# A fused two-block decoder kernel on one core: the top-k stage keeps the larger weight ring, its transposes and gate sums stand later, and the one-hots are laid out by four tokens

## The chip, the cores and the metric

The kernel runs on one NeuronCore of a Trainium2 chip. It is one launch. The metric is the time of one execution on the device in microseconds; less is better. TensorE (PE) does the matmuls, VectorE (DVE), ScalarE (ACT) and GpSimd (POOL) work beside it, and SyncE (SP) issues the transfers from memory.

## The reference, cut to what matters

The program is two transformer blocks over 256 tokens with 1024 channels. The change lies in the first block's feed-forward layer, which picks 16 of 16384 experts for each of 8 heads of a token:

```
q = (xt @ w_query).reshape(T, 8, 2, 128)
s = einsum('thpd,hpkd->thpk', q, subkeys)      # 128 scores per head and half
sv, si = lax.top_k(s, 16)
cand    = (sv[:, :, 0, :, None] + sv[:, :, 1, None, :]).reshape(T, 8, 256)
cand_id = (si[:, :, 0, :, None] * 128 + si[:, :, 1, None, :]).reshape(T, 8, 256)
top_s, pos = lax.top_k(cand, 16)
expert = take_along_axis(cand_id, pos, -1)
gate   = softmax(top_s, -1)
act = gelu(einsum('thkd,td->thk', u_tab[expert], xt), approximate=False)
out = einsum('thk,thkd->td', gate * act, v_tab[expert])
```

All of it is in float32.

## The kernel before, in words

The kernel gathers no experts. It computes the activations of all 16384 experts for all tokens (`peer_u`), builds from each token's 128 pairs of indices and gates a 128 x 128 matrix of gates (`peer_g`), multiplies the two, and multiplies the result with the whole value table (`peer_v`).

*Float32 on PE.* Each weight tile of 128 x 1024 comes by one transfer into a `raw` buffer; ACT rounds it into `hi` (L106), and DVE or POOL writes the rest, `lo = raw - hi` (L109). A product is three matmuls: hi with the high part of x, hi with the low part, lo with the high part (L255 to L257 in `ws`, where 256 tokens are the moving side; L196 to L198 and L898 with 512 columns). `lo_pattern` says which engine subtracts: `V` for DVE, `G` for POOL, `VG` in turns. The buffers stand in rings: 3 raw, 4 hi and 4 lo, and while `open_wx` holds the extra pool open 3 raw, 1 hi and 1 lo more.

*Stages around the change.* The output projection of the attention part ends with additions into `h` (L266), the norm of each token tile (L274 to L322), transposes (L334) and the split of x into xTh and xTl (L289). Then follow `peer_query` (about 142 to 190 us of the profiled span), the top-k stage (to 392), the gate stage (to 633), and the value stage in two calls of `peer_v` (to 815 and to 994). Ahead of `peer_query` the kernel closes the extra pool, and opens it again for the second call of `peer_v`.

*Top-k stage.* `merge` interleaves two generators by steps: `peer_topk` and `peer_u` for the first 64 of 128 groups of experts. A weight quarter is 128 x 2048, two halves of 24 matmuls each. All subtractions are POOL's here. For each token tile of 128 tokens, `peer_topk` computes scores (L749, four PSUM banks of the tag `sm`), picks 16 of 128 for sixteen head halves, adds candidates, picks 16 of 256 for eight heads (all DVE), and finds the indices of the picked by comparing with 0 to 15 (L792), multiplying with the indices (L795) and summing (L797). Then comes the gates' exponential (L800, ACT), their sum, reciprocal and product (L804 to L806, DVE), three transposes into one `sm` bank (L811 to L813), and copies into `sel` (L814, ACT) and `gate` (L815, DVE).

*Gate stage.* `peer_g` takes eight tokens at a time. Two one-hots E of shape [128 keys x 8 tokens], bf16, come from comparing `sel` with an iota (L852, DVE). For each four tokens ACT copies one into A (L857) and DVE multiplies the other with the gates into B (L858), both float32 in the storage of `h`. Four matmuls A x B give the gate matrices (L862), and L868 (DVE) and L870 (ACT) put them into the activations, which `peer_u` goes on computing for the experts 64 to 127 (L828, L830). In this stage and the value stage the subtractions alternate between DVE and POOL. The lines in which A and B are written are

```
A, B = [h[q].rearrange("p (n t j) -> p n t j", n=2, t=T2)[:, i] for q in range(2)]
a.activation(A, E[0][:, :, u:u + T2].rearrange("p j t -> p t j"), AF.Copy)
v.tensor_tensor(B, E[1][:, :, u:u + T2].rearrange("p j t -> p t j"),
                gate[:, t0:t0 + T2, None].to_broadcast([P, T2, P]), op=ALU.mult)
```

*Order of work.* Each engine runs its instructions in the order in which the tile scheduler puts them, and that order depends on the code's order, on the buffers, and on the scheduler's estimate of times.

## Time and profile before

| what | value |
|---|---|
| time, three runs | 1699.96, 1701.71, 1703.58 us (median 1701.71) |
| the profiled execution | 1688.16 us, its span 1686.3 us |
| granted TensorE clock, mean | 0.996 |
| PE busy | 1631.9 us, 97% |
| DVE busy | 1191.6 us, 71% |
| ACT busy | 948.1 us, 56% |
| POOL busy | 430.0 us, 25% |

The span goes from the first to the last instruction of the profiled execution; that execution's own time is 1.9 us longer. Waits of an engine are no busy time. Shares are means over all stages; the sections behind look at single stages.

### The profile page before, as it was taken

The page shows a single profiled execution, that of the slowest core. Times are in us where ns is not written, and L with a number is a line of the kernel's source. Part 1 is how long each engine was busy: PE and PEld are TensorE (multiplying, and loading weights), DVE is VectorE, ACT ScalarE, POOL GpSimd, SP SyncE. Part 2 cuts the span into 40 slices and gives each one's busy share as a digit, 9 for nine tenths or more (in the row PEclk, how much of TensorE's full clock was granted, in tenths as well). Part 3 has the DMA queues.
Part 4 walks back from the last instruction along what each step waited for, and adds up shares of the span by engine and source line. Part 5 has one row for each costly group of instructions (what it writes and reads, how often), then busy time and mean ns, then how long its engine had stood idle before and what let it go on. Part 6 is the DMA issues. An engine that isn't in the chain of part 4 may idle for free.

```text
span 1686.3 us, 27635 instructions
## 1 busy us (share of the span) xinstructions
PE 1631.9 (97%) x10592; PEld 1451.6 (86%) x10592; DVE 1191.6 (71%) x2236; ACT 948.1 (56%) x1435; POOL 430.0 (25%) x191
## 2 busy tenths in 40 slices
PE   6999999899999999999999999999999989999998
PEld 5878999899999997888888879869998777799986
DVE  7766597906999995445444467878885676688846
ACT  5544545446676665555455557466664556566633
POOL 1000598974332324444444411100000000000000
PEclk9999999999999999999999999999999999999999
DMA  7425655454444446566765555436555652365551
GB/s 272 159 88 162 198 157 173 161 175 156 145 135 141 133 144 203 185 193 201 232 194 187 188 177 178 131 113 197 183 193 186 216 174 87 119 196 189 188 188 62
DMA packets 83199, 285.07 MB, mean 169 GB/s; under 512 B 10555, under 2 KB 14588, under 8 KB 82940
## 3 DMA queue, kind: packets, MB, share of 16 engines
q1 hardware_dynamic: 83068, 283.31, 52.1%
q8 instruction: 83, 1.36, 0.3%
q14 instruction: 48, 0.39, 0.1%
HBM read 281.16 MB, written 2.12 MB: 168 GB/s over the span
## 4 chain that ended last, share of the span: by engine, by line
PE 70%; DVE 23%; ACT 2%; issue 1%; DMA 1%; POOL 1%; SPq 0%; DVEq 0%; ACTq 0%; POOLq 0%
PE mm L898 21%; PE mm L256 9%; PE mm L255 9%; PE mm L257 9%; PE mm L196 6%; PE mm L198 6%; PE mm L197 6%; DVE h L858 6%; DVE lo L109 4%; DVE E L852 3%; DVE act L868 2%; POOL lo L109 1%; PE sm L553 1%; DVE xn L322 1%; PE sm L525 1%
## 5 line engine op out<-in xcount | busy, mean ns | idle before, releaser
L106 ACT ACTIVATE hi<-raw 128x1024 fp32r<-128x1024 f32 x513 | 543.3, 1061 | 371.1 <-PE mm L256 156.4
L109 DVE TENSOR_TENSOR lo<-raw,hi 128x1024 fp32r<-128x1024 f32 x353 | 434.7, 1233 | 190.7 <-ACT hi L106 182.6
L255 PE MATMUL mm<-xTh,hi 128*128 128x256 f32 x1992 | 563.5, 283 | 0.0
L257 PE MATMUL mm<-xTh,lo 128*128 128x256 f32 x1992 | 556.5, 279 | 4.4 <-POOL lo L109 4.3
L256 PE MATMUL mm<-xTl,hi 128*128 128x256 f32 x1992 | 556.8, 280 | 0.7 <-DVE xTl L289 0.7
L109 POOL TENSOR_TENSOR lo<-raw,hi 128x1024 fp32r<-128x1024 f32 x160 | 406.2, 2545 | 423.7 <-ACT hi L106 423.5
L257 PEld LDWEIGHTS mm<-xTh,lo 128*128 128x128 f32 x1992 | 375.0, 188 | 5.6 <-POOL lo L109 5.4
L256 PEld LDWEIGHTS mm<-xTl,hi 128*128 128x128 f32 x1992 | 375.4, 188 | 1.3 <-DVE xTl L289 1.1
L255 PEld LDWEIGHTS mm<-xTh,hi 128*128 128x128 f32 x1992 | 375.3, 188 | 1.1 <-issue 0.6
L858 DVE TENSOR_TENSOR h<-E,gate 128x512 f32<-128x512 bf16 x64 | 115.2, 1800 | 4.3 <-PE sm L862 4.3
L196 PE MATMUL mm<-hi,xTh 128*128 128x512 f32 x256 | 105.6, 413 | 1.9 <-DVE xTl L289 1.0
L197 PE MATMUL mm<-lo,xTh 128*128 128x512 f32 x256 | 103.0, 402 | 0.5 <-DVE lo L109 0.5
L198 PE MATMUL mm<-hi,xTl 128*128 128x512 f32 x256 | 102.4, 401 | 0.0
L289 DVE TENSOR_TENSOR xTl<-act,xTh 128x256 fp32r<-128x256 f32 x64 | 45.1, 711 | 80.1 <-PE mm L898 78.9
L289 DVE TENSOR_TENSOR wl<-act,wh 128x256 fp32r<-128x256 f32 x64 | 43.3, 683 | 80.7 <-PE mm L898 80.4
L857 ACT ACTIVATE h<-E 128x512 f32<-128x512 bf16 x64 | 73.2, 1143 | 40.8 <-DVE E L852 39.2
L1320 DVE SCALAR_TENSOR_TENSOR fc<-mm,cw,fc 128x255 f32<-128x255 f32 (+1 forms) x176 | 84.5, 480 | 3.1
L898 PE MATMUL mm<-hi,xTh 128*128 128x512 f32 x256 | 81.0, 396 | 1.6 <-DVE act L828 0.9
L898 PE MATMUL mm<-hi,xTl 128*128 128x512 f32 x256 | 80.9, 396 | 0.1
L898 PE MATMUL mm<-lo,xTh 128*128 128x512 f32 x256 | 80.8, 395 | 0.0
L898 PE MATMUL mm<-hi,wh 128*128 128x512 f32 x256 | 80.2, 395 | 0.0
L898 PE MATMUL mm<-hi,wl 128*128 128x512 f32 x256 | 80.2, 395 | 0.0
(298 smaller groups left out, 2376.7 us busy)
## 6 DMA issues: line engine op xcount, KB each, us to landing
raw<-in_peer_uT SPq DMA_DIRECT2D x128, 512.0 KB, 3.7
raw<-in_peer_v SPq DMA_DIRECT2D x128, 512.0 KB, 4.4
raw<-in_ffn_up_ws SPq DMA_DIRECT2D x88, 512.0 KB, 3.7
raw<-in_ffn_down_a SPq DMA_DIRECT2D x40, 512.0 KB, 4.2
raw<-in_w_in_xs SPq DMA_DIRECT2D x20, 512.0 KB, 5.2
raw<-in_ab_ws SPq DMA_DIRECT2D x16, 512.0 KB, 4.4
raw<-in_ple_gate_xs SPq DMA_DIRECT2D x16, 512.0 KB, 4.5
raw<-in_w_query_ws SPq DMA_DIRECT2D x12, 512.0 KB, 4.8
```

Of the source, the lines that this page charges most:

```text
L106: nc.scalar.activation(hi, raw, AF.Copy)
L109: eng.tensor_tensor(lo, raw, f32(hi), op=ALU.subtract)
L196: nc.tensor.matmul(p, xh[:, k, t], hi[:, w], start=n == 1 and kk == 0, stop=False)
L197: nc.tensor.matmul(p, xh[:, k, t], lo[:, w], start=False, stop=False)
L198: nc.tensor.matmul(p, xl[:, k, t], hi[:, w], start=False, stop=n == total[c] and kk == 1)
L255: nc.tensor.matmul(o, hi[:, w], xh[:, k, :], start=k == 0, stop=False)
L256: nc.tensor.matmul(o, hi[:, w], xl[:, k, :], start=False, stop=False)
L257: nc.tensor.matmul(o, lo[:, w], xh[:, k, :], start=False, stop=k == 7)
L289: self.nc.vector.tensor_tensor(dl, p, f32(dh), op=ALU.subtract)
L858: v.tensor_tensor(B, E[1][:, :, u:u + T2].rearrange("p j t -> p t j"), gate[:, t0:t0 + T2, None].to_broadcast([P, T2, P]), op=ALU.mult)
L898: nc.tensor.matmul(self.acc[tt][c], st_[:, t], mv[:, c * 512:c * 512 + 512], start=first and j == js[0] and i == 0, stop=j == last and i == 2)
L1320: v.scalar_tensor_tensor(c[:, o + sft:o + S], p[:, o:o + S - sft], cw[:, wi, j:j + 1], c[:, o + sft:o + S], op0=ALU.mult, op1=ALU.add)
```

## The change

The extra pool of the weight ring is kept through `peer_query`, closed, opened again for the top-k stage (with the storage of the activations on the other side of memory), and closed ahead of the gate stage. The transposes of a token tile, the gate sums before them and the copies behind them move into a function `finish`: tile 0's is called in the seventh of tile 1's first sixteen steps, tile 1's after 14 steps more. In `peer_g` an E holds [2 groups][128 keys][4 tokens], so that the part of four tokens is contiguous; A and B are read in that order and written with a step of 128 float32. The two halves of the value stage change places, and its subtractions are all DVE's (`lo_pattern` is `V`). The diff, with the lines that only move cut from it:

```diff
--- before.py
+++ after.py
@@ -28,7 +28,8 @@
 NW_AB = 7
 HOLD = 4
 NWT = 6
-TOPK_STEPS = 90
+TOPK_STEPS = 74
+TOPK_REST = 14
 D_N = 3, 4
 D_PQ = 2
 LAG = 2
@@ -679,31 +680,34 @@
             px = e(self.tc.tile_pool(name="px", bufs=1, reuse_waits="tile"))
             xT = self.xT
             sel = px.tile([P, 2, S], BF, name="sel"), px.tile([P, S], F32, name="gate")
-            pa = e(self.pool("pa"))
-            self.slots = [pa.tile([P, 64, S], F32, name="act0")]
             keep = e(self.tc.tile_pool(name="keep", bufs=1, space=bass.MemoryType.DRAM)).tile([2, P, D], F32, name="keep")
             for t in range(2):
                 nc.sync.dma_start(keep[t], h[t])
-            self.close_wx()
-            with self.pool("topk") as tk:
-                qT = self.peer_query(xT, tk)
-                self.flush()
-                self.np.close()
-                self.merge(self.peer_topk(qT, tk, *sel), self.peer_u(xT, 0, 4))
-            self.acc = None
-            with self.pool("pg") as pg:
-                self.slots.append(pg.tile([P, 64, S], F32, name="act1"))
+            with ExitStack() as sa:
+                with self.pool("topk") as tk:
+                    qT = self.peer_query(xT, tk)
+                    self.flush()
+                    self.close_wx()
+                    self.np.close()
+                    pa = sa.enter_context(self.tc.tile_pool(name="pa", bufs=1, side="right", reuse_waits="tile"))
+                    self.slots = [pa.tile([P, 64, S], F32, name="act0")]
+                    self.open_wx()
+                    self.merge(self.peer_topk(qT, tk, *sel), self.peer_u(xT, 0, 4))
+                self.close_wx()
+                self.acc = None
+                self.slots.append(e(self.pool("pg")).tile([P, 64, S], F32, name="act1"))
                 self.done = [64, 0]
                 self.u_pattern = "VG"
                 with self.pool("gp") as gp:
                     self.merge(self.peer_g(*sel, gp), self.peer_u(xT, 4, 8))
+                self.lo_pattern = "V"
                 for t in range(2):
                     nc.sync.dma_start(h[t], keep[t])
-                self.run(self.peer_v(range(64, 128), xT))
+                self.run(self.peer_v(range(64), xT))
             self.open_norm()
             self.open_wx()
             pv = e(self.pool("pv"))
-            self.run(self.peer_v(range(64), [pv.tile([P, NWT, S], F32R, name=n) for n in ("wh", "wl")],
+            self.run(self.peer_v(range(64, 128), [pv.tile([P, NWT, S], F32R, name=n) for n in ("wh", "wl")],
                                  hold=4, norm=self.T["mix_norm"][0]))
 
     def act(self, j):
@@ -740,6 +744,19 @@
         nc.sync.dma_start(io, T["c_io16"])
         skT = big().rearrange("p (a k) -> p a k", a=16)
         nc.sync.dma_start(skT, T["subkeysT"])
+
+        def finish(tt, ij, gt, g3):
+
+            sm = self.tiny.tile([P, 8], F32, tag="gsm", name=self.nm("gsm"))
+            v.tensor_reduce(sm, g3, axis=AX.X, op=ALU.add)
+            v.reciprocal(sm, sm)
+            v.tensor_tensor(g3, g3, sm[:, :, None].to_broadcast([P, 8, 16]), op=ALU.mult)
+            p = self.sm_ps()
+            for i, x in enumerate((ij[:, :P], ij[:, P:], gt)):
+                self.tc.keep_in_program_order(nc.tensor.transpose(p[:, i * P:(i + 1) * P], x, self.ident))
+            t = slice(tt * P, tt * P + P)
+            a.activation(sel[:, :, t], p[:, :2 * P].rearrange("p (q t) -> p q t", q=2), AF.Copy)
+            v.tensor_copy(gate[:, t], p[:, 2 * P:3 * P])
         for tt in range(2):
             s = big()
             for b in range(4):
@@ -751,6 +768,8 @@
                 a.activation(s[:, b * 512:(b + 1) * 512], p, AF.Copy)
             sv, si = small(), small(U32)
             for hp in range(16):
+                if tt and hp == 6:
+                    finish(0, *late)
                 o, x = hp * 16, s[:, hp * P:(hp + 1) * P]
                 v.max(sv[:, o:o + 8], x)
                 v.max_index(si[:, o:o + 8], sv[:, o:o + 8], x)
@@ -795,24 +814,13 @@
                 v.tensor_tensor(e4, e4, sf4[:, :, q, None, :].to_broadcast([P, 8, 16, 16]), op=ALU.mult)
                 yield
                 v.tensor_reduce(ij[:, q * P:(q + 1) * P], e3, axis=AX.X, op=ALU.add)
+                if not q:
+                    self.tc.keep_in_program_order(a.activation(gt, gt, AF.Exp))
                 yield
-
-            self.tc.keep_in_program_order(a.activation(gt, gt, AF.Exp))
-            for _ in range(2):
-                yield
-            sm = self.tiny.tile([P, 8], F32, tag="gsm", name=self.nm("gsm"))
...
-            v.tensor_copy(gate[:, t], p[:, 2 * P:3 * P])
+            late = ij, gt, g3
+        for _ in range(TOPK_REST):
+            yield
+        finish(1, *late)
 
     def peer_u(self, xT, n0, n1):
 
@@ -841,22 +849,22 @@
 
         nc, h = self.nc, self.h
         v, a = nc.vector, nc.scalar
-        T1, T2 = 8, 4
-        iota = pool.tile([P, P, T1], BF, name="iota")
-        nc.gpsimd.iota(iota, pattern=[[1, P], [0, T1]], base=0, channel_multiplier=0, allow_small_or_imprecise_dtypes=True)
+        T1, T2 = 2, 4
+        iota = pool.tile([P, P, T2], BF, name="iota")
+        nc.gpsimd.iota(iota, pattern=[[1, P], [0, T2]], base=0, channel_multiplier=0, allow_small_or_imprecise_dtypes=True)
         yield S // T2
-        for b in range(S // T1):
-            t = slice(b * T1, b * T1 + T1)
-            E = [pool.tile([P, P, T1], BF, tag=f"E{q}", name=self.nm("E")) for q in range(2)]
+        for b in range(0, S, T1 * T2):
+            E = [pool.tile([P, T1, P, T2], BF, tag=f"E{q}", name=self.nm("E")) for q in range(2)]
             for q in range(2):
-                v.tensor_tensor(E[q], sel[:, q, None, t].to_broadcast([P, P, T1]), iota, op=ALU.is_equal)
-            for u in range(0, T1, T2):
-                i = u // T2
-                t0 = b * T1 + u
+                x = sel[:, q, b:b + T1 * T2].rearrange("p (n t) -> p n t", n=T1)
+                v.tensor_tensor(E[q], x[:, :, None, :].to_broadcast([P, T1, P, T2]),
+                                iota[:, None].to_broadcast([P, T1, P, T2]), op=ALU.is_equal)
+            for i in range(T1):
+                t0 = b + i * T2
                 A, B = [h[q].rearrange("p (n t j) -> p n t j", n=2, t=T2)[:, i] for q in range(2)]
-                a.activation(A, E[0][:, :, u:u + T2].rearrange("p j t -> p t j"), AF.Copy)
-                v.tensor_tensor(B, E[1][:, :, u:u + T2].rearrange("p j t -> p t j"),
-                                gate[:, t0:t0 + T2, None].to_broadcast([P, T2, P]), op=ALU.mult)
+                a.activation(A.rearrange("p t j -> p j t"), E[0][:, i], AF.Copy)
+                v.tensor_tensor(B.rearrange("p t j -> p j t"), E[1][:, i],
+                                gate[:, None, t0:t0 + T2].to_broadcast([P, P, T2]), op=ALU.mult)
                 p = self.bank("sm").rearrange("p (t j) -> p t j", t=T2)
                 for k in range(T2):
                     nc.tensor.matmul(p[:, k], A[:, k], B[:, k], start=True, stop=True)
```

The line numbers of the changed kernel are one higher up to L678, and some eight higher behind `peer_topk`: L322 becomes L323, L289 L290, L109 L110, L749 L766, L797 L816, L804 to L806 L751 to L753, L811 to L813 L756, L815 L759, L852 L860, L858 L866.

Three places of the instruction order are shown, each before and after. The first is DVE at the end of token tile 1's selection, in the kernel before:

```order
L792 TENSOR_TENSOR big_3569<-small_3501,io_1918 128x2048
L795 TENSOR_TENSOR big_3503<-big_3503,small_3300 128x2048
L795 TENSOR_TENSOR big_3569<-big_3569,small_3300 128x2048
L797 TENSOR_REDUCE small_3495<-big_3503 128x128
L797 TENSOR_REDUCE small_3495<-big_3569 128x128
L858 TENSOR_TENSOR h_79<-E_4277,gate 128x512
L852 TENSOR_TENSOR E_4362<-sel,iota 128x1024
L852 TENSOR_TENSOR E_4363<-sel,iota 128x1024
L804 TENSOR_REDUCE gsm_3673<-small_3496 128x8
L805 RECIPROCAL gsm_3673<-gsm_3673 128x8
L806 TENSOR_TENSOR small_3496<-small_3496,gsm_3673 128x128
L815 COPY gate<-sm_3702 128x128
```

And the same place in the changed kernel:

```order
L816 TENSOR_REDUCE small_3659<-big_3667 128x128
L816 TENSOR_REDUCE small_3659<-big_3734 128x128
L751 TENSOR_REDUCE gsm_4172<-small_3660 128x8
L752 RECIPROCAL gsm_4172<-gsm_4172 128x8
L753 TENSOR_TENSOR small_3660<-small_3660,gsm_4172 128x128
L860 TENSOR_TENSOR E_4280<-sel,iota 128x1024
L759 COPY gate<-sm_4176 128x128
L860 TENSOR_TENSOR E_4281<-sel,iota 128x1024
L866 TENSOR_TENSOR h_79<-E_4281,gate 128x128x4 x2
```

The gate stage's product L858 and two one-hots L852 stood between the reductions and the gate sums; now the sums stand directly behind the reductions, and the first one-hots of the gate stage behind them.

The second is PE where token tile 0's transposes and tile 1's first topk matmuls stand, in the kernel before:

```order
L256 MATMUL mm_2778<-xTl_71,hi_2781 128x256
L257 MATMUL mm_2778<-xTh_70,lo_2782 128x256
L811 MATMUL sm_2815<-ident,small_2633 128x128
L812 MATMUL sm_2815<-ident,small_2633 128x128
L813 MATMUL sm_2815<-ident,small_2634 128x128
L749 MATMUL sm_2822<-big_1920,qT_1436 128x128 x4
L749 MATMUL sm_2828<-big_1920,qT_1436 128x128 x4
```

In the changed kernel the topk matmuls of tile 1 stand without transposes ahead of them,

```order
L257 MATMUL mm_2839<-xTl_71,hi_2842 128x256
L258 MATMUL mm_2839<-xTh_70,lo_2843 128x256
L766 MATMUL sm_2877<-big_1923,qT_1431 128x128 x4
L766 MATMUL sm_2883<-big_1923,qT_1431 128x128 x4
L766 MATMUL sm_2889<-big_1923,qT_1432 128x128 x4
L766 MATMUL sm_2895<-big_1923,qT_1432 128x128 x4
L256 MATMUL mm_2839<-xTh_70,hi_2848 128x256
L257 MATMUL mm_2839<-xTl_71,hi_2848 128x256
```

and tile 0's transposes come 121 rows further down, each of the two index transposes in one row:

```order
L256 MATMUL mm_3015<-xTh_70,hi_3024 128x256
L257 MATMUL mm_3015<-xTl_71,hi_3024 128x256
L258 MATMUL mm_3015<-xTh_70,lo_3025 128x256
L756 MATMUL sm_3086<-ident,small_2735 128x128 x2
L756 MATMUL sm_3086<-ident,small_2736 128x128
L256 MATMUL mm_3097<-xTh_70,hi_3100 128x256
L257 MATMUL mm_3097<-xTl_71,hi_3100 128x256
```

The topk matmuls no longer have the transposes directly in front of them.

The third is DVE at the start of the query projection: h_78 is token tile 0 and h_79 tile 1, xn the normalised rows, mm_1234 the last bank of the output projection. Before:

```order
L284 SCALAR_TENSOR_TENSOR ry_1325<-rt_1326,ry_1325 128x1
L322 SCALAR_TENSOR_TENSOR xn_1338<-h_78,ry_1325,nw_1267 128x256
L322 SCALAR_TENSOR_TENSOR xn_1340<-h_78,ry_1325,nw_1267 128x256
L322 SCALAR_TENSOR_TENSOR xn_1342<-h_78,ry_1325,nw_1267 128x512
L109 TENSOR_TENSOR lo_1447<-raw_1444,hi_1446 128x1024
L289 TENSOR_TENSOR xTl_71<-sm_1344,xTh_70 128x2x128
L289 TENSOR_TENSOR xTl_71<-sm_1349,xTh_70 128x2x128
L289 TENSOR_TENSOR xTl_71<-sm_1354,xTh_70 128x4x128
L266 TENSOR_TENSOR h_79<-mm_1234,h_79 128x512
```

And now:

```order
L110 TENSOR_TENSOR lo_1461<-raw_1458,hi_1460 128x1024
L285 SCALAR_TENSOR_TENSOR ry_1325<-rt_1326,ry_1325 128x1
L267 TENSOR_TENSOR h_79<-mm_1234,h_79 128x512
L323 SCALAR_TENSOR_TENSOR xn_1338<-h_78,ry_1325,nw_1267 128x256
L323 SCALAR_TENSOR_TENSOR xn_1340<-h_78,ry_1325,nw_1267 128x256
L323 SCALAR_TENSOR_TENSOR xn_1342<-h_78,ry_1325,nw_1267 128x512
L290 TENSOR_TENSOR xTl_71<-sm_1344,xTh_70 128x2x128
L290 TENSOR_TENSOR xTl_71<-sm_1349,xTh_70 128x2x128
L275 SCALAR_TENSOR_TENSOR rx_1392<-ss_1387 128x1
```

The normalised rows of tile 0 stood ahead of the addition of the last bank, and now stand behind it.

## Rows read from the trace of the kernel before

**Rows 1.** The page: span, and busy time, share and instructions of each engine.

```profile
span 1686.3 us, 27635 instructions
...
PE 1631.9 (97%) x10592; PEld 1451.6 (86%) x10592; DVE 1191.6 (71%) x2236; ACT 948.1 (56%) x1435; POOL 430.0 (25%) x191
```

**Rows 2.** The page's chain that ended last: shares of the span by engine.

```profile
PE 70%; DVE 23%; ACT 2%; issue 1%; DMA 1%; POOL 1%; SPq 0%; DVEq 0%; ACTq 0%; POOLq 0%
```

**Rows 3.** Windows of the top-k stage: busy us (xinstructions) per engine, clock, DMA share, GB/s.

```profile
200.00:240.00 40.00, 40.00 (x345) 40.00 (x345) 39.93 (x145) 20.11 (x24) 36.72 (x14) 1.00 0.57 175
240.00:270.00 30.00, 26.56 (x224) 25.96 (x224) 19.73 (x30) 15.21 (x19) 25.46 (x9) 1.00 0.51 171
310.00:350.00 40.00, 31.73 (x253) 30.89 (x253) 29.87 (x13) 16.52 (x20) 36.07 (x12) 0.96 0.44 141
340.00:350.00 10.00, 10.00 (x76) 10.00 (x76) 0.29 (x1) 3.11 (x5) 6.07 (x3) 0.86 0.43 139
```

**Rows 4.** Waits of PE, window 240 to 275: us in total, times, longest.

```profile
PE sm L749 <- DVE gate L815: 2.0, 1, 2.0
```

**Rows 5.** Waits of PE, window 310 to 350.

```profile
PE sm L813 <- DVE small L806: 5.2, 1, 5.2
PE mm L257 <- POOL lo L109: 3.0, 3, 1.3
```

**Rows 6.** Timeline of DVE, token tile 1: start, duration, instruction, idle before it.

```profile
...
308.70 8.84 DVE L792 TENSOR_TENSOR big<-small,io 128x2048 f32<-128x2048 f32 x2
317.46 8.86 DVE L795 TENSOR_TENSOR big<-big,small 128x2048 f32<-128x2048 f32 x2
...
331.70 5.60 DVE L852 TENSOR_TENSOR E<-sel,iota 128x1024 bf16<-128x1024 bf16 x2
```

**Rows 7.** Timeline of POOL, the same stretch as rows 6.

```profile
308.28 33.59 POOL L109 TENSOR_TENSOR lo<-raw,hi 128x1024 fp32r<-128x1024 f32 x10 [1.72 <-ACT hi L106]
```

**Rows 8.** Windows of the gate stage, its first and its second half.

```profile
400.00:510.00 110.00, 110.00 (x952) 110.00 (x951) 104.27 (x148) 76.06 (x118) 33.61 (x14) 1.00 0.44 140
510.00:630.00 120.00, 119.15 (x1002) 116.70 (x1002) 120.00 (x156) 80.31 (x126) 38.55 (x16) 1.00 0.43 137
```

**Rows 9.** Groups by line: xcount, durations ns min/median/max, first and last start, forms.

```profile
L858 DVE TENSOR_TENSOR h<-E,gate x64: 1052/1088/3167, 307.7 to 627.1; 128x512 f32<-128x512 bf16 x64
...
L857 ACT ACTIVATE h<-E x64: 1118/1142/1171, 267.2 to 626.6; 128x512 f32<-128x512 bf16 x64
...
L1116 DVE TENSOR_TENSOR w<-v,v x6: 682/692/693, 1044.8 to 1078.8; 128x512 f32<-128x512 f32 x6
...
L852 DVE TENSOR_TENSOR E<-sel,iota x64: 656/679/2839, 264.7 to 622.5; 128x1024 bf16<-128x1024 bf16 x64
```

**Rows 10.** Groups by line, window 450 to 630, DVE: busy us, mean ns, idle before.

```profile
L868 DVE TENSOR_TENSOR act<-sm,act 128x256 f32<-128x256 f32 x48 | 19.9, 414 | 0.0
```

**Rows 11.** Timeline of DVE in the gate stage, two instructions a period apart.

```profile
...
557.66 2.95 DVE L858 TENSOR_TENSOR h<-E,gate 128x512 f32<-128x512 bf16 x1
...
565.44 2.95 DVE L858 TENSOR_TENSOR h<-E,gate 128x512 f32<-128x512 bf16 x1
```

**Rows 12.** Windows of the second half of the value stage.

```profile
815.00:994.00 179.00, 178.97 (x770) 144.21 (x768) 85.91 (x104) 93.60 (x126) 74.79 (x34) 1.00 0.59 188
```

**Rows 13.** Groups of subtractions by engine, window 815 to 994.

```profile
L109 DVE TENSOR_TENSOR lo<-raw,hi 128x1024 fp32r<-128x1024 f32 x34 | 43.1, 1268 | 8.9 <-ACT hi L106 6.0
```

**Rows 14.** Timeline of DVE at the start of the query projection.

```profile
...
138.69 1.55 DVE L322 SCALAR_TENSOR_TENSOR xn<-h,ry,nw 128x256 f32<-128x256 f32 x3
...
142.55 0.69 DVE L266 TENSOR_TENSOR h<-mm,h 128x512 f32<-128x512 f32 x1
```

**Rows 15.** Timeline of PE at the same place.

```profile
...
142.69 0.50 PE L196 MATMUL mm<-hi,xTh 128*128 128x512 f32 x1 [1.05 <-DVE xTl L289]
...
148.39 1.04 PE L334 MATMUL sm<-ident,xn 128*128 128x128 f32 x8
```

**Rows 16.** Timeline of PE at the start of the value stage.

```profile
639.15 0.47 PE L898 MATMUL mm<-hi,xTh 128*128 128x512 f32 x1 [0.91 <-DVE act L828]
```

11 lines of the change are left out of this document (removed).

## The prediction

> **What bounds the kernel now.** I read the page's first part before all else: TensorE is busy for 97% of the 1686.3 us span, VectorE for 71% [rows 1], and the chain that ended last lies on PE for 70% and on DVE for 23% [rows 2]. So time can be won only where PE stands still or issues below its pace, and that is to be found stage by stage. The windows show it as a count. In the top-k stage PE issues 345 matmuls in 40 us when nothing holds it, 8.625 per us; from 240 to 270 it issues 224 where that pace gives 258.75, and from 310 to 350 it issues 253 where it gives 345 [rows 3]. The missing 34.75 and 92 are 4.0 and 10.7 us: 14.7 us lost in this stage, at the two places where a token tile's selection ends.
>
> The lists of waits say to whom. At the first place 2.0 us go to a topk matmul (L749) that waits for the gate copy L815, because the PSUM bank that it wants still holds the transposes [rows 4]. At the second 5.2 us go to the transpose L813, which waits for the gates' multiplication L806 [rows 5]. Behind that idle time PE runs at a granted clock of 0.86 of full (a mean over both of its levels) from 340 to 350, and issues 76 instead of 86.25 [rows 3]: 1.2 us. What is left of the 14.7, 2.0 us at the first place and 4.3 at the second, is PE waiting for the subtractions that POOL makes; the list shows 3.0 us of it as waits of matmuls [rows 5], the rest lies in weight loads and short gaps.
>
> Why the gates came late is to be seen on DVE: after the two equality passes and the two products of tile 1 (17.7 us) come a gate product and two one-hots (5.6 us) of the gate stage, and only then the gates' sums and L806 [rows 6]. Why POOL came late: beside those passes ten subtractions took 33.59 us [rows 7], where alone they take 38.55/16 = 2.41 us each [rows 8]. In those 33.6 us PE wants 12.1 half weights (24 matmuls, 2.78 us, each) and gets ten.
>
> In the gate stage PE issues 952 in the first 110 us, and 1002 in the next 120 where that pace gives 1038.5: 36.5 missing, 4.2 us. DVE is busy for all 120 us of it [rows 8]. It bounds this half.
>
> **The change part by part.**
>
> *Transposes later.* Tile 0's transposes now stand some five weight quarters behind its reduction, tile 1's eight, and on DVE the sums and L806 (now L751 to L753) stand directly behind the reductions. A weight quarter is two halves, 5.6 us; 28 us and more for an exponential, three short DVE instructions and a copy hide everything that was waited for. The bank is free at the next topk matmul, since no transposes have used it. I take the whole 2.0 and 5.2 us, and the 1.2 us of slow clock that followed the idle time: **8.4 us**. The bounds are 7.2 (the clock dips for another reason) and 8.4.
>
> *Larger ring in the top-k stage.* One slot more for hi and lo lets POOL stand one half further ahead, three more raw slots let the transfers do so. One half is worth 2.78 us of PE's time, so the 2.0 us at tile 0 disappear, and of the 4.3 at tile 1 2.8 do: **4.8 us**. The ends are 0 (the lead isn't built up, because something else holds it back) and 6.3 (the lead is more than one slot, since the raws too are there earlier and the two one-hots of 5.6 us that slowed POOL have left the place).
>
> *The layout of the one-hots.* Before, ACT (A) and DVE (B) read every eighth bf16 of E, a step of 16 bytes, and wrote runs of 128; now they read 512 contiguous bf16 and write float32 512 bytes apart. B takes 1.09 us undisturbed and A 1.14; a contiguous two-input product of this size, L1116, takes 0.69 [rows 9]. No row shows a write of single elements a large step apart. From below B is bounded by 0.69. From above, if a scattered write costs as much as the scattered read did, it stays 1.09; if more, see the third rival. The nearest row is L868: it writes groups of four elements 1 KB apart, and reads its inputs with such jumps too, and 256 elements take 0.41 us [rows 10], which fits the 0.69 for 512 and leaves nothing for the jumps. So I take 0.69. The period of DVE for eight tokens is 7.78 us (from one B that meets POOL to the next) [rows 11], which at PE's full pace would be 7.52: 0.26 us too long. Two B's shorter by 0.40 each shed 0.8, and PE becomes the bound: **4.2 us**, with 0 and 4.2 as ends; B need only fall to 0.96. E keeps its count, its type and an unbroken write, so I leave it at 0.68; if its shorter inner run (four tokens, not eight) made it one element per step as L1116, it would take 1.38.
>
> The first E's now wait for the gates of tile 1 in DVE's order, and for the ring's slots, whose memory they take, and the iota (half as large) for POOL's last subtraction of the stage. Between tile 1's transposes and the first gate product PE has 72 weight matmuls queued, 8.3 us. Sel and gate copy, two E's at 0.68 and a B at 1.09 come to about 4 us [rows 9], so I cost it at nothing; without this cover it would be those 4 us, once.
>
> *Subtractions of the value stage to DVE.* PE is busy for 178.97 of 179 us of its second half, DVE for 85.9 [rows 12]. The subtractions that were POOL's, 64 in all, cost DVE 1.27 us each [rows 13]: about 41 us for each half, which makes 127 of 179. It stays under PE, so nothing; POOL's 75 us there fall away and nobody waited for them.
>
> *The order at the query's start.* This is a loss that the diff doesn't name. Before, the normalised rows of tile 0 are written at 138.69, ahead of the last h addition (142.55) [rows 14], and their transposes run between the last output-projection matmuls; the first query matmul starts at 142.69 after 1.05 us of idling [rows 15]. Now they stand behind that addition, which waits for the last projection matmul. Without the transposes (1.04 us for eight [rows 15]) the projection ends about 140.6 and the addition about 141.3; from the first normalised rows to the first query matmul it was 4.0 us, 1.2 of them a subtraction that has moved ahead, so that matmul comes about 144.1: 1.4 us later. For tile 1 the transposes came 5.8 us after the start of the addition; now three normalisations and three low parts (2.9 us) lie between, and they come at about 150, when the first group ends at 149.8 and the low parts must still follow: 0.8 us. Together **-2.2 us**, with 0 and -3 as ends.
>
> *Order of the halves in the value stage.* It begins with experts 0 to 63, whose activations were finished in the stage before; the wait of 0.91 us for the last products of the other slot (L828) [rows 16] goes: **0.9 us**.
>
> Sum: 8.4 + 4.8 + 4.2 - 2.2 + 0.9 = 16.1 us. The profiled execution took 1688.2 us, so it becomes 1672.1; it is 13.5 us under the median of the runs shown, 1701.7, and taking the same 16.1 from this gives **1685.6 us**.
>
> **Rivals.**
>
> *Scattered writes cost as scattered reads.* Then B stays 1.09, DVE keeps its period and the 4.2 us of the gate stage stay: 1701.7 - 11.9 = 1689.8 us. For it: the read with a 16-byte step does cost 0.40 us more than a contiguous one [rows 9]. Against it: L868 jumps for nothing, though after four elements, not one. [...]
>
> *The ring gives no lead.* If POOL is held back by ACT's hi copies and not by free slots, PE loses the 6.3 us again: 1701.7 - 11.3 = 1690.4 us. For it: PE's pace leaves POOL only 0.4 us per half to build a lead with. Against it: over the 40 us between the two places it gains a slot easily.
>
> *Slower: scattered writes are dearer than scattered reads.* DVE is full in the gate stage's second half, so whatever a B gains above 1.09 comes onto the path, 64 times. The rest of the gain is 11.9 us, so it decides at 1.09 + 11.9/64 = 1.28 us for a B. If the write pays twice the read's surcharge, B is 1.49: 25.6 us more, 1715 us. For it: a write touches a new place with each element, where the read touched one in every 16 bytes. Against it: L868 again.
>
> *New waits take the place.* The start of the query and the junction of top-k and gates together would have to cost 13 us or more, not 2.2, to leave no change, about 1699 us; the instructions in question last under 2 us each.
>
> **How the numbers follow.** The forecast 0.50, scattered writes as reads 0.18, no lead 0.10, dearer writes 0.15, new waits 0.07. The forecast's own range is 1681 to 1690. With the second and third cases and part of the last, 1680 to 1698 holds 8 in 10; below it nothing remains, since all terms at their upper ends give 19.8 us, 1681.9. A difference under 0.2% (3.4 us) can't be told from none here. Faster by more 0.78, within it 0.07, slower 0.15.
>
> **What would show it.** Right: PE's waits for L806 and L815 gone and the clock at 1.00 in the whole top-k stage; PE at 345 per 40 us there; B near 0.7 us, DVE under 100% and PE at 952 per 110 us in all of the gate stage; DVE about 70% busy in the value stage with PE's count unchanged; 1 to 2 us of idle PE at the query's start. Wrong: B at 1.1 or above with DVE full; POOL's subtractions still waited for; PE waiting for E or A at the first gate products; a longer value stage.

## The result, and the profile after

The changed kernel takes 1680.5 us, the median of five runs (1679.4 to 1682.5), and the one before 1700.0 (1695.7 to 1703.6): a ratio of 0.989, 95% interval 0.9868 to 0.9912, or 19.5 us less. The forecast was 1685.6, 16.1 us less.

The two profiled executions differ by 8.8 us only, 1686.3 and 1677.5 of span. The first of them was a lucky one of the kernel before: its granted clock was 0.996, where the runs of that kernel beside the experiments have 0.984 to 0.994. So stages are compared, and not spans. PE's timeline of the changed kernel shows where each begins: tile 1's transposes, the first topk matmul, the first gate product, the first matmul of the value stage (and one more there), and the transposes behind the value stage.

```profile
152.38 1.03 PE L335 MATMUL sm<-ident,xn 128*128 128x128 f32 x8
...
193.54 3.73 PE L766 MATMUL sm<-big,qT 128*128 128x128 f32 x32
...
379.56 1.05 PE L870 MATMUL sm<-h,h 128*128 128x128 f32 x8
...
618.62 0.73 PE L906 MATMUL mm<-hi,xTh 128*128 128x512 f32 x2 [0.27 <-ACT xTh L289]
...
623.42 0.47 PE L906 MATMUL mm<-hi,xTh 128*128 128x512 f32 x1 [0.97 <-DVE act L836]
...
980.01 0.83 PE L335 MATMUL sm<-ident,xn 128*128 128x128 f32 x4 [1.78 <-DVE xn L323]
```

The same starts in the kernel before, where tile 1's transposes stand in [rows 15]:

```profile
189.71 3.73 PE L749 MATMUL sm<-big,qT 128*128 128x128 f32 x32
...
392.16 1.05 PE L862 MATMUL sm<-h,h 128*128 128x128 f32 x8
...
634.37 0.73 PE L898 MATMUL mm<-hi,xTh 128*128 128x512 f32 x2 [0.66 <-ACT xTh L288]
...
995.75 0.83 PE L334 MATMUL sm<-ident,xn 128*128 128x128 f32 x4 [1.79 <-DVE xn L322]
```

| stage, by these starts | before, us | after, us | difference, us |
|---|---|---|---|
| up to the first topk matmul | 189.71 | 193.54 | +3.8 |
| top-k stage, to the first gate product | 202.45 | 186.02 | -16.4 |
| gate stage, to the first value matmul | 242.21 | 239.06 | -3.2 |
| value stage, to the transposes behind it | 361.38 | 361.39 | 0.0 |
| up to there | 995.75 | 980.01 | -15.7 |

The sum, -15.7, is within half a microsecond of the forecast's -16.1. Its terms are not. The page's busy times and the chain that ended last:

```profile
PE 1634.1 (97%) x10592; PEld 1455.7 (87%) x10592; DVE 1223.6 (73%) x2300; ACT 944.3 (56%) x1435; POOL 271.6 (16%) x127
...
PE 90%; DVE 7%; ACT 1%; issue 1%; DMA 1%; SPq 0%; DVEq 0%; ACTq 0%
```

PE now holds 90% of the chain, DVE 7% [rows 1, 2]. Windows of the top-k stage, as in [rows 3], and of the second half of the gate stage (cf. [rows 8]):

```profile
240.00:270.00 30.00, 30.00 (x262) 30.00 (x261) 21.36 (x19) 17.36 (x22) 30.00 (x11) 1.00 0.51 159
310.00:350.00 40.00, 40.00 (x348) 40.00 (x347) 21.43 (x10) 21.85 (x25) 39.60 (x15) 1.00 0.56 172
510.00:610.00 100.00, 99.85 (x854) 99.04 (x853) 100.00 (x132) 64.60 (x106) 31.16 (x13) 1.00 0.43 138
```

PE issues 262 matmuls from 240 to 270 and 348 from 310 to 350, where there were 224 and 253 [rows 3], at a clock of 1.00. In the last of the windows 854 where full pace gives 866: DVE is still busy for all of it. The waits for the gate copy and the gates' product [rows 4, 5] don't occur any more, and no matmul of the stage waits for POOL: PE's list of waits from 190 to 400 us is empty. But B and A, by line:

```profile
L866 DVE TENSOR_TENSOR h<-E,gate x64: 1044/1093/3242, 374.5 to 611.8; 128x512 f32<-128x512 bf16 x64
...
L865 ACT ACTIVATE h<-E x64: 1109/1140/1164, 373.7 to 611.4; 128x512 f32<-128x512 bf16 x64
```

take 1.09 and 1.14 us as they did [rows 9]. And the start of the query projection, on PE's timeline, with the window of 140 to 150 as last row:

```profile
141.66 0.74 PE L335 MATMUL sm<-ident,xn 128*128 128x128 f32 x4 [1.38 <-DVE xn L323]
142.62 0.66 PE L335 MATMUL sm<-ident,xn 128*128 128x128 f32 x4 [0.22 <-DVE xn L323]
...
145.13 0.50 PE L197 MATMUL mm<-hi,xTh 128*128 128x512 f32 x1 [1.85 <-DVE ry L278]
...
145.85 0.63 PE L199 MATMUL mm<-hi,xTl 128*128 128x512 f32 x1
146.28 0.63 PE L197 MATMUL mm<-hi,xTh 128*128 128x512 f32 x1
...
140.00:150.00 10.00, 6.54 (x24) 4.69 (x23) 8.90 (x24) 3.42 (x8) 0.00 (x0) 0.83 0.82 265
```

PE idles 1.4, 0.2 and 1.9 us, where it idled 1.05 [rows 15], and then issues eight matmuls about 0.43 us apart instead of 0.23, at a mean clock of 0.83 of the window. Tile 1's transposes come at 152.38, not at 148.39. On DVE a subtraction stands ahead of the last of tile 0's low parts:

```profile
143.26 1.22 DVE L110 TENSOR_TENSOR lo<-raw,hi 128x1024 fp32r<-128x1024 f32 x1
144.40 0.68 DVE L290 TENSOR_TENSOR xTl<-sm,xTh 128x512 fp32r<-128x512 f32 x1
```

That low part ends at 145.08 and the first query matmul starts at 145.13, as it started 0.06 us behind the last low part before (142.63 and 142.69); the `ry` that the row names comes next on DVE. The value stage begins with the same kind of wait as before, 0.97 us for L836 (L828 before) [rows 16].

### The profile page after: what moved, and what is told of

Read it like the earlier page. It is cut to its first block, busy times and chain, and to the rows that moved or that the text cites. A ratio compares the mean times of both kernels' runs of the same rounds, so it can differ in the third digit from the quotient of the medians.

```text
span 1677.5 us, 27611 instructions
## 1 busy us (share of the span) xinstructions
PE 1634.1 (97%) x10592; PEld 1455.7 (87%) x10592; DVE 1223.6 (73%) x2300; ACT 944.3 (56%) x1435; POOL 271.6 (16%) x127
## 4 chain that ended last, share of the span: by engine, by line
PE 90%; DVE 7%; ACT 1%; issue 1%; DMA 1%; SPq 0%; DVEq 0%; ACTq 0%
PE mm L906 21%; PE mm L256 14%; PE mm L257 14%; PE mm L258 14%; PE mm L197 6%; PE mm L199 6%; PE mm L198 6%; PE sm L870 3%; DVE lo L110 2%; PE sm L554 1%; DVE xn L323 1%; PE sm L335 1%; PE sm L526 1%; PE sm L1136 1%; DVE h L267 1%
## 5 line engine op out<-in xcount | busy, mean ns | idle before, releaser
L110 DVE TENSOR_TENSOR lo<-raw,hi 128x1024 fp32r<-128x1024 f32 x417 | 511.8, 1229 | 199.2 <-ACT hi L107 194.3
L110 POOL TENSOR_TENSOR lo<-raw,hi 128x1024 fp32r<-128x1024 f32 x96 | 248.9, 2611 | 243.2 <-ACT hi L107 227.7
L866 DVE TENSOR_TENSOR h<-E,gate 128x512 f32<-128x512 bf16 x64 | 115.5, 1808 | 1.9 <-PE sm L870 1.9
L860 DVE TENSOR_TENSOR E<-sel,iota 128x1024 bf16<-128x1024 bf16 x64 | 48.5, 796 | 44.9 <-POOL iota L854 39.6
L906 PE MATMUL mm<-lo,wh 128*128 128x512 f32 x256 | 80.2, 395 | 0.0
```

Source lines behind the costliest of these rows:

```text
L110: eng.tensor_tensor(lo, raw, f32(hi), op=ALU.subtract)
L866: v.tensor_tensor(B.rearrange("p t j -> p j t"), E[1][:, i], gate[:, None, t0:t0 + T2].to_broadcast([P, P, T2]), op=ALU.mult)
L906: nc.tensor.matmul(self.acc[tt][c], st_[:, t], mv[:, c * 512:c * 512 + 512], start=first and j == js[0] and i == 0, stop=j == last and i == 2)
```

## Experiments

Each changes the changed kernel, unless it says otherwise. Times are medians; ratios are to runs of the kernel before on the same chip. Stages are named as in the table above.

### The ring in the query projection

```diff
+            self.close_wx()
             with ExitStack() as sa:
                 with self.pool("topk") as tk:
                     qT = self.peer_query(xT, tk)
                     self.flush()
-                    self.close_wx()
```

> The changed kernel, but the extra pool is closed ahead of the query projection as before, and opened only for the top-k stage. Theory: the larger ring lets subtractions and the last addition stand ahead of the normalised rows of tile 0 on DVE, PE idles, and its clock falls. Then the stretch from tile 0's norm to the first topk matmul, 57.3 us in the changed kernel and 53.3 in the one before, is back at 53.3, PE's clock there is 1.00, and the whole is 4 us shorter than the changed kernel (about 1676.5 us beside 1680.5). Rival: the order there comes from the other storage of the activations, or the loss from the transfers; then the stretch stays near 57 us. Second rival: the early raws were needed, and the top-k stage takes longer than its 186.0 us.

1679.2 us, ratio 0.987 (0.985 to 0.989). PE's timeline has tile 1's transposes and the first topk matmul at

```profile
148.34 1.04 PE L335 MATMUL sm<-ident,xn 128*128 128x128 f32 x8
...
189.66 3.73 PE L766 MATMUL sm<-big,qT 128*128 128x128 f32 x32
```

so the loss of 3.9 us is undone, and the top-k stage takes 186.2 us: the early raws were not needed. The theory held for the stages. Other traces have the same: with the larger ring in the query projection PE idles 1.4, 0.2 and 1.9 us there (the changed kernel, gates_V, contiguous_writes, old_layout, early_finish, small_ring_topk), and with the smaller one only once, for 1.04 to 1.05 us (the two traces of the kernel before, small_ring_query, both). The median fell by 1.3 us only, on another chip; the rest can't be told from the spread of the runs (1677.0 to 1682.3).

### No POOL in the gate stage

```diff
-                self.u_pattern = "VG"
+                self.u_pattern = "V"
```

> The changed kernel, but in the gate stage DVE makes all subtractions and POOL none. Theory: what fills DVE there is not the product B itself (1.09 us) but the B in each period of eight tokens that meets a subtraction of POOL and takes 3.0 us; without POOL DVE sheds 32 x 1.95 = 62 us and takes on 32 x 1.21 = 39, so it is no longer full, PE runs at its pace throughout, and the stage from the first to past the last gate product takes 237.3 us (32 periods of 7.415) instead of 239.1; all in all 1 to 2 us shorter. Rival: the long B's have another cause; then DVE has 39 us more to do in a full stage, and the kernel is 30 us or more longer.

1676.4 us, ratio 0.985 (0.983 to 0.986). The gate products by line, and the window 510 to 610:

```profile
L866 DVE TENSOR_TENSOR h<-E,gate x64: 1067/1088/1242, 373.6 to 608.3; 128x512 f32<-128x512 bf16 x64
...
510.00:610.00 100.00, 100.00 (x866) 100.00 (x865) 95.39 (x148) 68.92 (x108) 0.00 (x0) 1.00 0.48 145
```

No B is longer than 1.24 us, DVE is busy for 95% instead of all, and PE issues 866 matmuls. The gate stage takes 237.2 us, as expected. The value stage takes 1.6 us less as well (359.8): with DVE no longer behind, the wait at its start is gone. Together that is more than the 1 to 2 us expected of the whole. So what filled DVE was the B that runs beside a subtraction of POOL: in the changed kernel 3.02 us at 550.91, where POOL subtracts from 550.58 to 552.98, and 1.08 us at 548.04, where POOL is idle.

### A and B written without a step

Here the gate products read their rows in another order, so that part of the computation is changed.

```diff
-                a.activation(A.rearrange("p t j -> p j t"), E[0][:, i], AF.Copy)
+                a.activation(A, E[0][:, i].rearrange("p j t -> p (j t)").rearrange("p (t j) -> p t j", t=T2), AF.Copy)
...
-                v.tensor_tensor(B.rearrange("p t j -> p j t"), E[1][:, i],
+                v.tensor_tensor(B.rearrange("p t j -> p (t j)").rearrange("p (j t) -> p j t", t=T2), E[1][:, i],
```

> The changed kernel, but A and B are written without a step, in the order in which E lies; so the gate products read rows of another order, and this part of the computation is changed. Theory: the scattered write is what holds B at 1.09 us and A at 1.14; then B is 0.69 to 0.75 us undisturbed, A about 0.6, DVE isn't full and the gate stage takes 237.3 us. Rival: the write costs nothing, and B is held by its operands (bf16, or the gate read in runs of four); then it stays at 1.09 us and the stage at 239.1.

1678.8 us, ratio 0.986 (0.984 to 0.988), the gate stage 237.2 us, as the theory had it. By line:

```profile
L866 DVE TENSOR_TENSOR h<-E,gate x64: 673/682/2785, 376.7 to 609.6; 128x512 f32<-128x512 bf16 x64
...
L865 ACT ACTIVATE h<-E x64: 608/622/637, 375.9 to 609.1; 128x512 f32<-128x512 bf16 x64
```

B falls to 0.68 us and A to 0.62. So the scattered write costs 0.41 us of a B and 0.52 of an A; since both took the same 1.09 and 1.14 us before, that is all that the contiguous read had saved.

### The old layout of the one-hots

The edit puts the function `peer_g` of the kernel before in place of the new one.

> The changed kernel with the one-hots, A and B laid out as before (E over eight tokens, read with a step of 16 bytes, written contiguous). Theory: the new layout makes a B's place on DVE 0.09 us shorter (the next instruction starts 0.91 us after it instead of 1.00, while its own record stays at 1.09), and that is what shortened the gate stage where DVE is full; then a period there is 7.78 us instead of 7.70 and the stage about 1.3 to 3 us longer, 240.4 to 242. Rival: the stage is shorter because of how it is entered, and the layout is worth nothing; then 239.1.

1685.0 us (1677.5 to 1688.3), ratio 0.991 (0.989 to 0.993); the gate stage takes 241.3 us against 239.1. DVE's timeline over one period, the changed kernel first:

```profile
548.04 1.08 DVE L866 TENSOR_TENSOR h<-E,gate 128x512 f32<-128x512 bf16 x1
548.95 0.34 DVE L876 TENSOR_TENSOR act<-sm,act 128x176 f32<-128x176 f32 x1
...
550.91 3.02 DVE L866 TENSOR_TENSOR h<-E,gate 128x512 f32<-128x512 bf16 x1
...
558.65 2.99 DVE L866 TENSOR_TENSOR h<-E,gate 128x512 f32<-128x512 bf16 x1
```

and with the old layout:

```profile
548.85 1.09 DVE L866 TENSOR_TENSOR h<-E,gate 128x512 f32<-128x512 bf16 x1
549.83 0.35 DVE L876 TENSOR_TENSOR act<-sm,act 128x176 f32<-128x176 f32 x1
...
551.79 2.96 DVE L866 TENSOR_TENSOR h<-E,gate 128x512 f32<-128x512 bf16 x1
...
559.63 2.92 DVE L866 TENSOR_TENSOR h<-E,gate 128x512 f32<-128x512 bf16 x1
```

The next instruction starts 0.91 us after an undisturbed B in the one and 0.98 in the other (0.97 to 1.00 over neighbouring periods), and the period (from one long B to the next) is 7.74 against 7.84 us. The theory held. The layout gives 2.2 us of the 3.2 of this stage; the other microsecond isn't explained by it.

### The ends of the tiles where they stood before, with the larger ring

The edit puts `peer_topk` of the kernel before in place of the new one, with its 90 steps.

> The changed kernel with the larger ring, but the exponential, the gate sums, the transposes and the copies stand where they stood before. Theory as in the prediction: the late transposes are worth 8.4 us (2.0 for the topk matmul that waits for the bank, 5.2 for the transpose that waits for the gates' product, 1.2 of slow clock after it), so the top-k stage takes 194 us instead of 186.0. Rival: the 5.2 us came from the gate product and one-hots that stood ahead of the sums on DVE, and the larger ring, whose memory the one-hots take, keeps them away by itself; then only the wait for the bank (2.0) and a short wait for the sums (0 to 2) return, and the stage takes 188 to 190 us.

1680.8 us, ratio 0.990 (0.987 to 0.993), and the top-k stage takes 186.2 us: as long as with the late transposes. Its windows:

```profile
240.00:270.00 30.00, 30.00 (x262) 30.00 (x261) 26.87 (x50) 17.82 (x23) 30.00 (x10) 1.00 0.50 160
310.00:350.00 40.00, 40.00 (x346) 40.00 (x345) 19.16 (x9) 21.40 (x25) 40.00 (x15) 1.00 0.56 179
```

PE is full, and has no wait for the bank or the gates' product. Neither number held. The rival's way was right and went further: the wait for the bank is gone too. This called for the other half.

### Late transposes without the larger ring

```diff
                     self.slots = [pa.tile([P, 64, S], F32, name="act0")]
-                    self.open_wx()
                     self.merge(self.peer_topk(qT, tk, *sel), self.peer_u(xT, 0, 4))
-                self.close_wx()
```

> The changed kernel with the larger ring in the query projection but not in the top-k stage (the extra pool isn't opened again there). Theory: PE's waits for POOL's subtractions come back, 6.3 us of them, and the stage takes 192 us instead of 186.0, while nothing waits for the sums or for the bank. Rival: the late transposes alone give POOL the time, since PE's own stops at the transposes no longer bunch the work; then the stage stays within 1 us of 186.

1699.4 us, ratio 1.0002 (0.998 to 1.002): the whole gain is gone. The stage takes 204.6 us, more than the 192 expected. Waits of PE in its timeline, and then of ACT:

```profile
321.44 0.38 PE L256 MATMUL mm<-xTh,hi 128*128 128x256 f32 x1 [3.68 <-ACT hi L107]
...
332.13 0.58 PE L258 MATMUL mm<-xTh,lo 128*128 128x256 f32 x1 [10.20 <-POOL lo L110]
...
318.55 1.98 ACT L863 ACTIVATE h<-E 128x512 f32<-128x512 bf16 x2 [10.45 <-DVE E L858]
...
335.69 1.06 ACT L107 ACTIVATE hi<-raw 128x1024 fp32r<-128x1024 f32 x1 [11.45 <-DMA raw<-in_peer_uT]
```

PE waits 3.7 and 10.2 us. On ACT the first product A (L863) waits 10.5 us for a one-hot on DVE, with the hi copies of the next weights queued behind it; the raw slots stay taken, and ACT then idles 11.5 us for the next transfer. So the larger ring seems to do something that the prediction named without a price of its own: its memory is that of the one-hots, and it keeps the gate stage's work out of the top-k stage. DVE's timelines agree. The first one-hot of the kernel before, and that of the changed one, which waits for the `iota` behind POOL's last subtraction of the stage:

```profile
264.70 2.47 DVE L852 TENSOR_TENSOR E<-sel,iota 128x1024 bf16<-128x1024 bf16 x1
...
372.94 0.69 DVE L860 TENSOR_TENSOR E<-sel,iota 128x1024 bf16<-128x1024 bf16 x1 [39.59 <-POOL iota L854]
```

### Which part of the ring

In four kernels a pad tile that lasts to the end of the stage takes the memory of the slots left out, so that no one-hot starts early. The number of slots more in raw, hi and lo differs; in the first

```diff
                     self.open_wx()
+                    self.xr = dict(raw=3, hi=0, lo=0)
+                    self.pad = self.wx.tile([P, 2048], F32, name="pad")
+                    nc.vector.memset(self.pad[:, :1], 0.0)
...
         finish(1, *late)
+        v.tensor_copy(self.pad[:, 1:2], gate[:, S - 1:S])
```

and the others have 0, 1, 1 (hilo_only) and 0, 0, 0 (kept_out and kept_out_early). kept_out_early has `peer_topk` of the kernel before, and the pad's last use at that function's end.

> The changed kernel, with three raw slots more in the top-k stage as it has, but no hi and no lo slot more; a pad tile takes their memory, so that the one-hots of the gate stage still can't start early. First theory (the prediction's): the one slot more of hi and lo is POOL's lead, and without it PE waits for subtractions again, some 4 to 6 us; the top-k stage takes 190 to 192 us instead of 186.0. Rival: what held POOL back was ACT, waiting for raw tiles whose transfer couldn't be issued before POOL had freed a slot (45.8 us of such waits in the kernel before, none in the changed one); then the raws alone give everything, and the stage takes 186 to 187 us.

> The counterpart: one hi and one lo slot more in the top-k stage, raw slots three as before, a pad in the memory of the others. First theory: the lead of one half is there, the stage takes 186 to 187 us. Rival (raws): with three raw slots a transfer waits for POOL, hi for the transfer, POOL for hi; a slot more behind that loop gives at most its own 2.8 us, and PE still waits; 189 to 193 us, with ACT waiting for raw tiles 30 us or more.

> No slot more in the top-k stage, only a pad tile in the memory that the slots would take, so that no one-hot, A or B of the gate stage can be made before the stage's end; transposes late, as in the changed kernel. The kernel without pad and without slots was as slow as the one before, and PE stood still for 15 us there, 10.2 of them at once, while ACT waited for a one-hot with hi copies queued behind it. Theory: that long wait is the gate stage's work intruding, so it goes, and only PE's waits for POOL remain, 4 to 6 us; the top-k stage takes 190 to 192 us. Rival: the waits come from the ring's lack of slots alone; then the stage takes 199 us or more as before.

> The same pad without slots, but with the exponential, sums, transposes and copies where they stood before. It differs from the kernel before (in this stage) in the one thing that gate-stage work can't stand ahead of the sums. Theory: the 5.2 us wait for the gates' product was that work (one product and two one-hots, 5.6 us beside POOL), so it shrinks to 0 to 2 us, while the waits for the bank (2.0) and for POOL (4 to 6) stay; the stage takes 193 to 196 us instead of 202.5. Rival: the sums come late because the reductions do; then the wait of 5 us stays and the stage takes 200 us or more.

| kernel | transposes | slots more (raw, hi, lo) | first one-hot, us after the stage's start | top-k stage, us | gate stage, us | median, us | ratio (95%) |
|---|---|---|---|---|---|---|---|
| before | early | none | 75 | 202.5 | 242.2 | 1700.0 | 1 |
| small_ring_topk | late | none | 119 | 204.6 | 239.6 | 1699.4 | 1.000 (0.998 to 1.002) |
| kept_out_early | early | none (pad) | 153 | 198.4 | 241.2 | 1693.6 | 0.996 (0.994 to 0.999) |
| kept_out | late | none (pad) | 192 | 194.1 | 242.6 | 1690.8 | 0.994 (0.992 to 0.996) |
| raws_only | late | 3, 0, 0 (pad) | 187 | 190.9 | 241.7 | 1689.5 | 0.994 (0.992 to 0.995) |
| hilo_only | late | 0, 1, 1 (pad) | 188 | 190.0 | 242.4 | 1686.4 | 0.992 (0.989 to 0.994) |
| early_finish | early | 3, 1, 1 | 180 | 186.2 | 239.0 | 1680.8 | 0.990 (0.987 to 0.993) |
| after | late | 3, 1, 1 | 179 | 186.0 | 239.1 | 1680.5 | 0.989 (0.987 to 0.991) |

Stage times are from one trace each; the top-k stages of two traces of the kernel before differ by 1.2 us. In kept_out_early the pad ends with tile 1's gates, so there the one-hots stay away from the sums, but not to the stage's end. The pads of the other three hold them back to within 2 to 4 us of the stage's end, the larger ring to within 6 to 7. Part of what a pad wins is lost behind it: over the top-k and gate stages together small_ring_topk takes 444.2 us, kept_out 436.7 and the changed kernel 425.1.

The waits from 190 to 385 us, in total, times and longest: of the kernel before,

```profile
ACT hi L106 <- DMA raw<-in_peer_uT: 45.8, 24, 3.3
```

of kept_out_early,

```profile
ACT hi L108 <- DMA raw<-in_peer_uT: 60.1, 34, 3.5
...
PE mm L259 <- POOL lo L111: 4.5, 3, 1.9
...
PE sm L758 <- DVE gate L824: 2.7, 1, 2.7
```

of kept_out,

```profile
ACT hi L109 <- DMA raw<-in_peer_uT: 74.0, 43, 3.6
...
PE mm L260 <- POOL lo L112: 4.1, 4, 1.3
```

of hilo_only,

```profile
ACT hi L109 <- DMA raw<-in_peer_uT: 65.2, 38, 3.3
```

of raws_only,

```profile
PE mm L260 <- POOL lo L112: 2.6, 2, 1.3
```

and of the changed kernel:

```profile
ACT hi L107 <- PE mm L257: 49.3, 29, 2.1
```

With three raw slots ACT waits 46 to 74 us for transfers; with six (raws_only and the changed kernel) no such wait is listed, and ACT waits for PE instead. The raws alone take off 3.2 of the 8.1 us between kept_out and the changed kernel, hi and lo alone 4.1. So raws_only came out as its first theory's stage time had it (190.9 of 190 to 192, though with 2.6 us of waits for POOL instead of 4 to 6), and hilo_only as its rival had it: each half of the slots gives part of the 8.1 us, and neither gives all. kept_out took 194.1 us, 2 more than expected, with PE's waits for POOL as expected (4.1). In kept_out_early the wait for the gates' product is gone, as the theory had it, and that for the bank stays (2.7), which with the slots (early_finish) is gone; the stage takes 2.4 us more than expected. Its first one-hots fall into the stage: up to 385 us DVE waits 2.4 us for the `iota` and ACT 3.7 us for an E, waits that kept_out's list doesn't have; so the 4.3 us between these two kernels aren't the transposes' alone.

### Both improvements, and the kernel before once more

> The changed kernel with both improvements of the first experiments: the extra pool closed during the query projection, and no subtractions on POOL in the gate stage. Theory: the two lie in different stages and add up. The stretch to the first topk matmul is 3.9 us shorter, the gate stage 1.8, the start of the value stage 1.6: 7.3 us off the profiled span of 1677.5 and the median near 1673 us. Rival: one of them takes the place of the other, since PE's head start into the gate stage changes where DVE is late; then 1676.

1673.5 us (1669.0 to 1676.4), ratio 0.985 (0.982 to 0.988). Its stages are 186.2, 237.2 and 359.8 us, and it reaches the transposes behind the value stage at 972.03, 8.0 us ahead of the changed kernel: they add up, as the theory had it. PE is full in the second half of the gate stage:

```profile
510.00:610.00 100.00, 100.00 (x866) 100.00 (x864) 93.80 (x148) 67.86 (x107) 0.00 (x0) 1.00 0.45 147
```

> The kernel before once more, for a second trace of it. Its profiled execution took 1688 us at a mean granted clock of 0.996, its other runs some 1700 at 0.984 to 0.990. Theory: those runs lose the difference to PE's slow clock in stages that the change leaves alone, behind the value stage; then this trace has the same stage times up to there within 1 us (top-k stage 202.5, gate stage 242.2, value stage 361.4) and loses some 8 to 12 us behind it where the clock is below 1.00. Rival: the loss lies in the top-k stage, where PE's long waits let the clock fall for longer than in the first trace; then that stage takes 208 us or more, and the change gains more there than the first trace shows.

1699.3 us. The same stages take 203.6, 242.0 and 361.5 us, and the transposes come at 995.96. From there to the end it takes 697.2 us, where the first trace took 690.5 and the changed kernel 697.5. The window in which most of that lies, in the first trace and in this one:

```profile
1360.00:1480.00 120.00, 113.20 (x626) 91.83 (x627) 83.53 (x260) 67.59 (x152) 0.00 (x0) 0.97 0.39 124
...
1360.00:1480.00 120.00, 112.93 (x567) 91.58 (x568) 81.56 (x258) 64.47 (x148) 0.00 (x0) 0.91 0.36 115
```

The clock's mean is 0.97 in the one and 0.91 in the other. The theory held, with 6.7 us rather than 8 to 12 and with 1.1 us of difference in the top-k stage. Over all traces of this case the stretch behind the value stage takes 690.5 to 699.1 us, and that before the top-k stage differs too: in raws_only, hilo_only and small_ring_topk the first topk matmul comes at 199.2 to 199.4, and in small_ring_topk the clock's mean is 0.74 from 80 to 100 us, where the changed kernel has 1.00.

## Why the prediction was right, point by point

- **Transposes later, 8.4 us.** The step that failed. The 2.0, the 5.2 and the 1.2 us did go, but the late transposes were not needed for it. With the larger ring the early transposes give the same 186 us; without it the late ones give nothing. The wait for the gates' product was the gate stage's work ahead of the sums, as [rows 6] showed it (its 5.60 us are the two one-hots alone; with the product it is 6.75), and the ring's memory keeps that work away. Only with neither slots nor intruding work are late transposes worth something, at most 198.4 - 194.1 = 4.3 us. I read from the order of the changed kernel that the sums stand behind the reductions, and put it down to `finish`.
- **Larger ring, 4.8 us.** Mis-sized: alone it is worth 16.2 us of the stage (202.5 to 186.2). With late transposes keeping the one-hots out takes off 10.4 us (204.6 to 194.1) and the slots 8.1; with early ones, and a pad that ends sooner, it is 4.0 and 12.2. Counted over the top-k and gate stages the first pair is 7.4 and 11.7, so the split is rough; that both parts count is not. The prediction counted a half of lead for hi and lo. That the one-hots would wait for the ring's memory it said itself, but it saw in that no gain beyond POOL's subtractions; and that the transfers held ACT back (45.8 us in the stage before) it named as a thing three raw slots could do, but did not price.
- **Layout, 4.2 us.** The value taken for B, 0.69, was wrong: the first rival's 1.09 is what was measured, and the row that I took as nearest (L868, runs of four) doesn't tell what single elements cost. A B takes 1.09 us when it writes scattered and 0.68 when it writes contiguous (contiguous_writes). The stage still gained 3.2 us, 2.2 of them with the layout, where the instruction behind a B starts about 0.07 us earlier. The period at PE's full pace was off too: 237.2 us for 32 of them are 7.41 us each, not 7.52, so an unburdened DVE is worth 5.0 us in this stage.
- **Subtractions of the value stage to DVE, nothing.** Right: 361.4 us in both. DVE is busy for 94.3 us from 800 to 960, 59% and not about 70%, since its other low parts got shorter with POOL idle: 0.43 us (L290), from a mean of 0.72 (L289), which from 820 to 850 was 0.42 to 0.43 alone and 0.95 to 1.03 beside a subtraction of POOL.
- **The query's start, -2.2.** Right in place and mechanism, mis-sized: -3.8. The first query matmul came at 145.13 (forecast 144.1), since a subtraction of 1.2 us, which the forecast took to have moved ahead, still stands before the last low part; the slow clock behind the idle time, about 1.5 us (eight matmuls 0.43 us apart instead of 0.23), was not in the sum; and the 0.8 us for tile 1 didn't occur.
- **Order of the halves, 0.9.** Wrong: 0. The wait is for L836 (L828 before) whichever half comes first, and goes only when DVE isn't behind (gates_V, contiguous_writes). The premise was wrong as well: in the code L876 multiplies gates into the activations of experts 0 to 63 up to the end of the gate stage, so they are not finished in the stage before. L836 reads a PSUM bank of the tag `mm`, the tag of the value stage's accumulators; whether that bank is what the matmul waits for I did not test.
- The sum came out at 15.7 us in the stages by luck, since the errors cancel: 3.2 more in the top-k stage, 1.0 less in the gate stage, 1.6 and 0.9 less elsewhere. The median moved by 19.5; in later stages the change leaves the code alone, and how much of the other 3.8 is the clock there stays open. With them the result, 1680.5, lies below the forecast's own range (1681 to 1690) and the 1681.9 below which nothing should remain, and half a microsecond inside the 1680 to 1698 that was to hold 8 in 10.

## What to carry to other kernels

A larger buffer ring does two things: it lets producers run ahead, and it keeps whatever would have used that memory from starting early. Where an early start of the next stage lands in the queues ahead of the present stage's work, that can be worth about as much as the slots. Before a gain is split among the parts of a change, each part is to be run alone: here the sum was right and the split was not.

An engine that is full only because its instructions run longer beside another's (here a B on DVE, 3.0 us beside a subtraction of POOL and 1.09 without) can be relieved by giving it *more* work, taken from the other (gates_V: DVE busy for 95% of the window instead of all).

## What the runs showed of the hardware

- Writing 512 single float32 values 512 bytes apart takes 1.09 us on DVE and 1.14 on ACT, contiguous 0.68 and 0.62. Reading bf16 with a step of 16 bytes and writing contiguous, in the kernel before, took 1.09 and 1.14 us too. Groups of four, 1 KB apart, cost nothing that shows (L868: 0.41 us for 256, beside 0.68 for the 512 contiguous ones).
- Two records of 1.08 and 1.09 us can take different places on DVE: the next instruction starts 0.91 us after the one (the changed kernel at 548.04), 0.98 after the other (old_layout at 548.85).
